# First mixer's projections taken two chunks at a time, with their weights loaded as halves of the rows

## The chip, the cores and the metric

The kernel runs on one core of one Trainium2 chip. The metric is device time in microseconds (us): three runs of the kernel before took 1580.92, 1581.1 and 1586.4 us, and their median, 1581.1 us, is the time before. One more execution was taken by the hardware profiler: it took 1579.73 us, of which 1578.0 us lie between its first and its last instruction (the span). All profile rows below come from that execution.

## The reference, cut to what matters

Two layers of a hybrid decoder run over 592 tokens at once: 16 meta tokens, 64 sample tokens (8 sequences of 8) and 512 prompt tokens. Layer 0 is an RMSNorm, one combined input projection, a group of four mLSTM heads and a group of four retention heads, an output projection, and a ConvFFN; layer 1 has another mixer. Only layer 0's input projection is touched here:

```
q_a, k_a, v_a, o_a, i_a, f_a, q_b, k_b, v_b, g_gate = split_cols(xn @ w_in, AB_SIZES)
...
xs_b = (rotary(heads(q_b, H_B), pos), rotary(heads(k_b, H_B), pos) * DK_B ** -0.5, heads(v_b, H_B))
state_b, h_b = run_blocks(ret_step, state_b, xs_b, CHUNK_B, prompt)
h_b = jax.nn.silu(g_gate.astype(jnp.float32)) * head_layer_norm(h_b, g_b)
```

`w_in` has 1024 rows and 4104 columns of four bytes. Each head of q, k, o, and of the second group's q, k and gate, has 128 columns; v has 128 columns for each head too, and i and f have four columns each.

## The kernel before, in words

Features lie on the 128 partitions and tokens on the free axis, so that activations are eight tiles of 128 x 592 (`state[0]` to `state[7]`). Every fp32 operand is kept as two tiles, a high part rounded to the fp32r format and a low part, the rest, and each product is three matmuls: high by high, high by low, low by high.

**Weights.** `raw_weights` (L346) loads a piece of a weight matrix into one of two buffers called `wr`; a piece is 512 KB in this layer. A `Split` (L281) makes of it the high part `wh` (a cast on ScalarE, L302) and the low part `wl` (a subtraction on VectorE, L306), each in one of three buffers. A `wr` buffer is free again when its `wl` has been made; a `wh` and a `wl` are free when TensorE has read them for the last time. `pump` (L321) keeps up to three pieces made and not yet used up, and `done` (L315) gives one back and makes the next. `stream` (L325) runs the dense blocks in the order of a list, and fetches ahead until two more pieces are on their way:

```
def pump():
    while line and len(live) < 3:
        line[0].get()
...
def fetch():
    while sum(len(w or ()) for w, _ in ahead) < 2:
...
S.copy(hi, src)
...
V.tensor_tensor(out=lo, in0=src, in1=hi.bitcast(F32), op=ALU.subtract)
```

**Projections.** `proj` (L417) makes one chunk of 128 output features: one piece of weights (1024 rows, 128 columns: each row of the piece is 512 bytes in memory), eight steps of `dense` (L390) of six matmuls each into one PSUM tile `dp`, and then a `post` that takes the sum out of PSUM. There are 24 such chunks in this layer: `q_`, `k_`, `o_`, `qb`, `kb` and `g_`, for four heads each. `token_proj` (L424) makes v, for two heads at once, tokens on the partitions; its weights come as two pieces of 512 rows and 256 columns (1024 bytes a row), and its results are taken out of PSUM by ScalarE, one tile of tokens at a time (L938, and L1021 for the gates' columns). There are two PSUM tiles of the size that `dp` and `tp` use.

**Mixers.** Each head has a generator, `mixer_a` (L1150) or `mixer_b` (L1245), which starts when its q and k are there (`mixer_b`: its v too) and adds its small matmuls between those of the dense blocks; at most two run at a time (`interleave`, L133). The `post` of `qb` and `kb` is `post_rot` (L1136): two copies out of PSUM on ScalarE into `sw` (L1139, L1140), then three operations on VectorE (L1142 to L1144); the last writes the k of the head, which `mixer_b` transposes on TensorE as the first thing it does (L1255, the tile `p0`). Heads of the second group are called b0 to b3 below, and those of the first a0 to a3.

**What sets the order.** The list `blocks` in `layer0` (L1314 to L1317) is written by hand. A recording layer turns the program into one in-order list of instructions for each engine, and moves instructions of the mixers between those of the dense blocks. Loads are issued from SyncE's queue (SP), which also issues the stores of states (`out_C`, `out_R`) and the loads of states (`s_s`), in order; each waits there for its buffer. ScalarE and VectorE are in order as well: a cast that waits for its load holds up what stands behind it.

Of the kernel before, what the change touches and what calls it, by code (L numbers as in the profile page):

```python
# [23 lines left out]
NT = NMETA + NSAM + NP  # L24
# [75 lines left out]
def trunk_kernel(ctx: ExitStack, tc: tile.TileContext, I, O):  # L100
# [8 lines left out]
    dp = ctx.enter_context(tc.tile_pool(name="dp", bufs=1, space=bass.MemoryType.DRAM))  # L109
# [7 lines left out]
    def matmul(out, lhsT, rhs, **kw):  # L117
        n = 1
        for d in rhs.shape[1:]:
            n *= d  # L120
        m = lhsT.shape[1]
        clock[0] += max(n, 64) / 2.4 + 3 if rhs.dtype == F32R else max(2 * n, 2 * m, 64) / 1.2
        T.matmul(out, lhsT=lhsT, rhs=rhs, **kw)  # L123
# [38 lines left out]
    def tmp(name, n=NT, dt=F32):  # L162
        return tp.tile([128, n], dt, name=name, tag="t", bufs=4)
# [10 lines left out]
    def mm(name):  # L174
        return pp.tile([128, 1024], F32, name=name, tag="mm", bufs=2)
# [29 lines left out]
    state = {"x": "xa", "h": "xb", "ssq": {}}  # L205
# [153 lines left out]
    def weights(*views):  # L359

        return [Split(r.shape[1], r.shape[2], r) for r in map(raw_weights, views)]

    def got(ws):
        return [sp.get() for sp in ws]
# [23 lines left out]
    OFF = {0: (216, 296), 14: (208, 304), 16: (208, 304)}  # L388

    def dense(ws, acts, c0=0, hooks=None, span=None):  # L390


        off, mid = OFF[c0]
        halves = [(c0, mid), (mid, NT)] if span is None else [span]
        if span is not None:
            off = -span[0]
        ps = [mm("dp") if span is None else px("dq") for _ in ws]
        nk = len(acts)
        for k in range(nk):
            xh, xl = acts[k]  # L400
            for p, (hi, lo) in zip(ps, ws):
                for i, (ww, xx) in enumerate(((hi, xh), (hi, xl), (lo, xh))):
                    for a, b in halves:
                        matmul(p[:, off + a:off + b], lhsT=ww[:, k, :], rhs=xx[:, a:b], start=k == 0 and i == 0,
                               stop=k == nk - 1 and i == 2)
            if hooks and k in hooks:
                hooks[k]()
            yield
        return ps, off

    def cols(w, c0, n=128):
        return w.rearrange("(k p) n -> p k n", p=128)[:, :, c0:c0 + n]

    def acts_x():
        return [state[c] for c in range(8)]

    def proj(w, c0, post, first=0, hooks=None):  # L417

        def body(ww):
            (p,), off = yield from dense(got(ww), acts_x(), first, hooks)  # L420
            post(p[:, off + first:off + NT])
        return (lambda: weights([cols(w, c0)]), body)

    def token_proj(w, pieces, emit, first=False, hook=None, chunks=None):  # L424

# [56 lines left out]
    def slot(kind, j, dt=F32):  # L482
        return ap.tile([128, NT], dt, name=f"{kind}{j}", tag=f"{kind}{j}")
# [51 lines left out]
    def action(f):  # L535
        def body(_):
            f()
            yield
        return (lambda: None, body)
# [393 lines left out]
    def emit_v(name):  # L933

        def f(t, r, p):
            if t == 0:
                vs[name] = vtile("v_" + name)
            S.activation(vs[name][:r, t, :, 0:128], p[:r, 0:256].rearrange("p (h d) -> p h d", d=128), AF.Copy,  # L938
                         scale=state["rt"][:r, t:t + 1])
            if t == 4:  # L940
                gates["v" + name] = True
        return f

    def gate_tile():
        return tp.tile([128, NT], F32, name="gate", tag="gate", bufs=4)

    def silu_gate(name, first=0):

        def post(p):
            z = tmp("gz")  # L950
            if first:
                G.memset(z[:, 0:first], 0.0)
            V.tensor_tensor(out=z[:, first:], in0=p, in1=state["rb"][:, first:], op=ALU.mult)
            g = gate_tile()
            S.activation(g, z, AF.Tanh, scale=0.5)
            V.scalar_tensor_tensor(out=g, in0=g, scalar=1.0, in1=z, op0=ALU.add, op1=ALU.mult)
            gates[name] = g
        return post
# [19 lines left out]
    def layer0():  # L978
        w = I["w_in_ab"][0]
# [32 lines left out]
        def emit_va(hp):  # L1012
            f0 = emit_v(f"a{hp}")

            def f(t, r, p):
                f0(t, r, p)
                if t == 0:
                    if hp == 0:
                        G.memset(gt, 0.0)
                    G.memset(vs[f"a{hp}"][:, :, :, 128:129], 1.0)  # L1020
                S.activation(gt[:r, t, 32 * hp:32 * hp + 4], p[:r, 256:260], AF.Copy, scale=state["rt"][:r, t:t + 1])  # L1021
            return f
# [91 lines left out]
        def post_q(h):  # L1114
            def f(p):
                q = slot("bh", h)
                V.tensor_tensor(out=q, in0=p, in1=state["rb"], op=ALU.mult)
                qk["q", h] = q
            return f

        def post_k(h):
            def f(p):
                k = slot("bl", h)
                V.scalar_tensor_tensor(out=k, in0=p, scalar=128 ** -0.5, in1=state["rb"], op0=ALU.mult, op1=ALU.mult)
                qk["k", h] = k
            return f

        def post_o(h):
            def f(p):
                g = gate_tile()  # L1130
                V.tensor_tensor(out=g, in0=p, in1=state["rb"], op=ALU.mult)
                S.activation(g, g, AF.Tanh, scale=0.5)
                gates["a", h] = g
            return f

        def post_rot(h, sc, kind, key):  # L1136
            def f(p):
                sw = tmp("sw")
                S.copy(sw[0:64, :], p[64:128, :])  # L1139
                S.copy(sw[64:128, :], p[0:64, :])  # L1140
                t1 = slot(kind, 4 + h)
                V.scalar_tensor_tensor(out=t1, in0=p, scalar=sc, in1=cosr, op0=ALU.mult, op1=ALU.mult)  # L1142
                V.scalar_tensor_tensor(out=sw, in0=sw, scalar=sc, in1=sinr, op0=ALU.mult, op1=ALU.mult)
                V.tensor_tensor(out=t1, in0=t1, in1=sw, op=ALU.add)  # L1144
                qk[key, 4 + h] = t1
            return f
# [98 lines left out]
        def mixer_b(h):  # L1245
# [54 lines left out]
            for t, (t0, r) in enumerate(TILES[1:]):  # L1300
# [3 lines left out]
            S.copy(nums[:, 1:5, 0:128], quad(na))  # L1304
            mixed[4 + h] = yield from head_out(nums, epst[:, h, :], gate_mul, 4 + h, gnh[:, 4 + h:5 + h], True, ("b", h))

        q_ = lambda h: proj(w, 128 * h, post_q(h))
        k_ = lambda h: proj(w, 512 + 128 * h, post_k(h))
        o_ = lambda h: proj(w, 1536 + 128 * h, post_o(h))
        qb = lambda h: proj(w, 2056 + 128 * h, post_rot(h, 1.0, "bh", "q"))  # L1310
        kb = lambda h: proj(w, 2568 + 128 * h, post_rot(h, 128 ** -0.5, "bl", "k"))
        g_ = lambda h: proj(w, 3592 + 128 * h, silu_gate(("b", h)))
        vb = lambda hp: token_proj(w, [(3080 + 256 * hp, 256)], emit_v(f"b{hp}"))
        blocks = [token_proj(w, [(1024, 256), (2048, 4)], emit_va(0), first=True, chunks=start),  # L1314
                  token_proj(w, [(1280, 256), (2052, 4)], emit_va(1), hook=norm_bcast), action(setup),
                  q_(0), k_(0), q_(1), k_(1), o_(0), q_(2), k_(2), o_(1), q_(3), k_(3), o_(2), vb(0),
                  qb(0), kb(0), o_(3), qb(1), kb(1), g_(0), vb(1), qb(2), kb(2), g_(1), qb(3), kb(3), g_(2), g_(3)]  # L1317
        streams = [rows()] + [mixer_a(h) for h in range(4)] + [mixer_b(h) for h in range(4)]
        return blocks, streams, mixed

# [302 lines left out]
    def finish(a, b):  # L1623
# [22 lines left out]
        for c in range(0, 8, 2):  # L1646
# [5 lines left out]
            ld.dma_start(out=O["y"][:, c:c + 2, a - NMETA:b - NMETA], in_=y)  # L1652

    b0, s0, mix0 = layer0()
    b1, s1, mix1 = layer1()
    blocks = b0 + mix_proj(I["w_out_ab"][0], mix0, 0, V_NFFN, xin)
# [65 lines left out]
```

## Time and profile before

| | |
|---|---|
| median of three runs | 1581.1 us (1580.92 to 1586.4) |
| the profiled execution | 1579.73 us |
| its span | 1578.0 us |
| TensorE matmuls busy | 1530.4 us, 97% of the span |
| weight loads into TensorE busy | 1483.8 us, 94% |
| VectorE busy | 1148.9 us, 73% |
| ScalarE busy | 730.9 us, 46% |
| GpSimd busy | 194.2 us, 12% |
| mean granted TensorE clock | 0.992 of full speed |

A busy share is an average over stages with different limits. The first mixer takes about the first 305 us of the span; the 24 projections lie between 47 and 302 us. To see what a change in it can be worth, one reads what TensorE waited for in that stretch, which engine ended each wait, and what that engine had waited for before. Idle time is given in brackets before an instruction, with what ended it.

### The profile page before, as it was taken

What the parts mean: (1) busy time and instruction counts of PE and PEld (TensorE: products, weight loads), DVE (VectorE), ACT (ScalarE), POOL (GpSimd) and SP (SyncE); (2) the same over time, 40 slices, a digit from 0 to 9 for tenths busy, and PEclk for the clock granted to TensorE, in tenths of its full rate; (3) what the DMA queues carried; (4) which work ended last, traced back from release to release, by engine and by line L of the source; (5) the groups of instructions that cost most, each with busy time, mean ns of one, the idle gap of its engine ahead of it and who ended that gap; (6) DMA issues with size and microseconds to landing.
All of it is one profiled execution on the core that took longest, in us unless ns stands there. A gap on an engine that the chain in (4) does not pass through costs nothing. (4 is left out here: it accounts for less than half of the span.)

```text
span 1578.0 us, 32152 instructions
## 1 busy us (share of the span) xinstructions
PE 1530.4 (97%) x13100; PEld 1483.8 (94%) x13100; DVE 1148.9 (73%) x2359; ACT 730.9 (46%) x1325; POOL 194.2 (12%) x399
## 2 busy tenths in 40 slices
PE   7999999999999999999998899999999999999996
PEld 7999998999999999999998798898999999999995
DVE  6576573758988877777556776766689887888875
ACT  6443343335444444444355556564454444444453
POOL 2000000001210000110004525333012000000001
PEclk9999999999999999999999999999999999999998
DMA  6654556423322232223422132123333223233234
GB/s 185 98 98 87 92 101 64 132 82 100 89 80 82 83 93 81 86 88 118 152 81 67 57 97 99 57 97 99 98 99 94 81 81 93 82 95 93 69 108 131
DMA packets 217812, 148.57 MB, mean 94 GB/s; under 512 B 7704, under 2 KB 209176, under 8 KB 217664
## 3 DMA queue, kind: packets, MB, share of 16 engines
q1 hardware_dynamic: 217664, 146.51, 34.7%
q8 instruction: 103, 1.69, 0.4%
q14 instruction: 45, 0.37, 0.1%
HBM read 131.84 MB, written 14.65 MB: 93 GB/s over the span
## 5 line engine op out<-in xcount | busy, mean ns | idle before, releaser
L302 ACT CAST wh<-wr 128x1024 fp32r<-128x1024 f32 (+3 forms) x238 | 230.7, 970 | 394.1 <-PE dp L123 118.5
L306 DVE TENSOR_TENSOR wl<-wr,wh 128x1024 fp32r<-128x1024 f32 (+3 forms) x238 | 267.9, 1126 | 75.4 <-ACT wh L302 73.2
L123 PE MATMUL dp<-h,wh 128*128 128x296 f32 (+1 forms) x1088 | 242.4, 304 | 0.7 <-ACT v_c L938 0.5
L123 PE MATMUL dp<-xl,wh 128*128 128x296 f32 (+1 forms) x1088 | 236.6, 298 | 0.0
L123 PE MATMUL dp<-h,wl 128*128 128x296 f32 (+1 forms) x1088 | 236.4, 298 | 0.0
L123 PE MATMUL dp<-bh,wh 128*128 128x296 f32 (+2 forms) x864 | 188.4, 299 | 0.8 <-DVE x L511 0.5
L123 PE MATMUL dp<-bh,wl 128*128 128x296 f32 (+2 forms) x864 | 186.5, 297 | 0.0
L123 PE MATMUL dp<-bl,wh 128*128 128x296 f32 (+2 forms) x864 | 186.4, 297 | 0.0
L123 PEld LDWEIGHTS dp<-h,wh 128*128 128x128 f32 x1088 | 174.5, 189 | 4.3 <-issue 1.8
L123 PEld LDWEIGHTS dp<-xl,wh 128*128 128x128 f32 x1088 | 176.7, 189 | 0.0
L123 PEld LDWEIGHTS dp<-h,wl 128*128 128x128 f32 x1088 | 176.3, 188 | 0.0
L123 PEld LDWEIGHTS dp<-bh,wh 128*128 128x128 f32 x864 | 139.0, 188 | 3.1 <-issue 1.4
L123 PEld LDWEIGHTS dp<-bh,wl 128*128 128x128 f32 x864 | 139.5, 188 | 0.0
L123 PEld LDWEIGHTS dp<-bl,wh 128*128 128x128 f32 x864 | 139.4, 188 | 0.0
L123 PE MATMUL ac<-h,wh 128*128 128x296 f32 (+1 forms) x408 | 123.3, 302 | 2.6 <-DVE cs L724 2.6
L123 PE MATMUL ac<-h,wl 128*128 128x296 f32 (+1 forms) x408 | 121.5, 298 | 0.0
L123 PE MATMUL ac<-xl,wh 128*128 128x296 f32 (+1 forms) x408 | 121.3, 297 | 0.0
L123 PE MATMUL tp<-wh,h 128*128 128x256 f32 (+3 forms) x280 | 82.8, 300 | 12.8 <-ACT wh L298 6.0
L615 ACT ACTIVATE cv<-cv 128x612 f32<-128x612 f32 (+1 forms) x44 | 31.1, 708 | 116.9 <-DVE cv L611 116.9
L302 ACT CAST wh<-s 128x1024 fp32r<-128x1024 f32 x68 | 56.8, 835 | 59.0 <-PE sb L123 34.7
L123 PEld LDWEIGHTS ac<-h,wh 128*128 128x128 f32 x408 | 76.9, 188 | 5.1 <-DVE cs L724 3.9
L123 PE MATMUL sb<-b2h,wl 128*128 128x296 f32 (+1 forms) x272 | 81.0, 298 | 0.0
(475 smaller groups left out, 3431.9 us busy)
## 6 DMA issues: line engine op xcount, KB each, us to landing
wr<-in_w_ffn_in SPq DMA_DIRECT2D x88, 512.0 KB, 3.8
wr<-in_w_ffn_out SPq DMA_DIRECT2D x32, 512.0 KB, 3.5
wr<-in_w_in_c SPq DMA_DIRECT2D x32, 512.0 KB, 3.9
wr<-in_w_in_ab SPq DMA_DIRECT2D x30, 512.0 KB, 7.6
wr<-in_w_ffn_out SPq DMA_DIRECT2D x24, 384.0 KB, 3.5
x<-in_x SPq DMA_DIRECT2D x16, 296.0 KB, 4.2
out_H<-s_s SPq DMA_DIRECT2D x8, 576.0 KB, 2.8
wr<-in_w_out_ab SPq DMA_DIRECT2D x16, 256.0 KB, 2.7
```

Of the source, the lines that this page charges most:

```text
L123: T.matmul(out, lhsT=lhsT, rhs=rhs, **kw)
L302: S.copy(hi, src)
L306: V.tensor_tensor(out=lo, in0=src, in1=hi.bitcast(F32), op=ALU.subtract)
L615: S.activation(env_["cv"][:, b0:612], env_["cv"][:, b0:612], AF.Silu)
```

## The change

A new function `proj_pair` takes two neighbouring chunks, 256 columns, as one block. Their weights come as two pieces as before, but cut the other way: the upper 512 rows and the lower 512 rows, 256 columns each, so that a row of a piece is 1024 bytes. The pieces stay 512 KB, the casts and subtractions stay of the same size and number (24 each), and so do the matmuls. The first chunk goes through the steps 0 to 7. The second goes through 4 to 7 and then 0 to 3, so that the piece of the steps 4 to 7 is used up after three quarters of the block, where `done` gives it back. Both pieces must be made before the block's instructions are written down; on the chip, the matmuls of a step wait only for the piece that they read.

The list of blocks follows: the heads of q, k, o, qb, kb and g now come in pairs of heads (0, 1) and (2, 3), so that q of head 1 comes before k of head 0, and so on; `vb(0)` stays behind k of head 3 but moves ahead of o of head 2, and `vb(1)` stands behind the gates of heads 0 and 1.

```
--- before.py
+++ after.py
@@ -420,6 +420,27 @@
             (p,), off = yield from dense(got(ww), acts_x(), first, hooks)
             post(p[:, off + first:off + NT])
         return (lambda: weights([cols(w, c0)]), body)
+
+    def proj_pair(w, c0, posts):
+
+
+        def body(ws):
+            halves = got(ws)
+            off, mid = OFF[0]
+            for i, ks in enumerate((range(8), (4, 5, 6, 7, 0, 1, 2, 3))):
+                p = mm("dp")
+                for k in ks:
+                    hi, lo = (w_[:, k % 4, 128 * i:128 * i + 128] for w_ in halves[k // 4])
+                    xh, xl = state[k]
+                    for j, (ww, xx) in enumerate(((hi, xh), (hi, xl), (lo, xh))):
+                        for a, b in ((0, mid), (mid, NT)):
+                            matmul(p[:, off + a:off + b], lhsT=ww, rhs=xx[:, a:b], start=k == ks[0] and j == 0,
+                                   stop=k == ks[-1] and j == 2)
+                    if i and k == 7:
+                        ws[1].done()
+                    yield
+                posts[i](p[:, off:off + NT])
+        return (lambda: weights(*[[cols(w, c0, 256)[:, k0:k0 + 4, :]] for k0 in (0, 4)]), body)
 
     def token_proj(w, pieces, emit, first=False, hook=None, chunks=None):
 
@@ -1304,17 +1325,17 @@
             S.copy(nums[:, 1:5, 0:128], quad(na))
             mixed[4 + h] = yield from head_out(nums, epst[:, h, :], gate_mul, 4 + h, gnh[:, 4 + h:5 + h], True, ("b", h))
 
-        q_ = lambda h: proj(w, 128 * h, post_q(h))
-        k_ = lambda h: proj(w, 512 + 128 * h, post_k(h))
-        o_ = lambda h: proj(w, 1536 + 128 * h, post_o(h))
-        qb = lambda h: proj(w, 2056 + 128 * h, post_rot(h, 1.0, "bh", "q"))
-        kb = lambda h: proj(w, 2568 + 128 * h, post_rot(h, 128 ** -0.5, "bl", "k"))
-        g_ = lambda h: proj(w, 3592 + 128 * h, silu_gate(("b", h)))
+        def two(c0, post):
+            return lambda h: proj_pair(w, c0 + 128 * h, [post(h), post(h + 1)])
+
+        q_, k_, o_ = two(0, post_q), two(512, post_k), two(1536, post_o)
+        qb = two(2056, lambda h: post_rot(h, 1.0, "bh", "q"))
+        kb = two(2568, lambda h: post_rot(h, 128 ** -0.5, "bl", "k"))
+        g_ = two(3592, lambda h: silu_gate(("b", h)))
         vb = lambda hp: token_proj(w, [(3080 + 256 * hp, 256)], emit_v(f"b{hp}"))
         blocks = [token_proj(w, [(1024, 256), (2048, 4)], emit_va(0), first=True, chunks=start),
                   token_proj(w, [(1280, 256), (2052, 4)], emit_va(1), hook=norm_bcast), action(setup),
-                  q_(0), k_(0), q_(1), k_(1), o_(0), q_(2), k_(2), o_(1), q_(3), k_(3), o_(2), vb(0),
-                  qb(0), kb(0), o_(3), qb(1), kb(1), g_(0), vb(1), qb(2), kb(2), g_(1), qb(3), kb(3), g_(2), g_(3)]
+                  q_(0), k_(0), o_(0), q_(2), k_(2), vb(0), qb(0), o_(2), kb(0), g_(0), vb(1), qb(2), kb(2), g_(2)]
         streams = [rows()] + [mixer_a(h) for h in range(4)] + [mixer_b(h) for h in range(4)]
         return blocks, streams, mixed
 
```

Three places show how it moves instructions. The first is SyncE's queue from the last state stores of the heads b0 and b1 on. Before, `wr_2722`, `wr_2724`, `wr_2877`, `wr_2939`, `wr_3001`, `wr_3186` and `wr_3262` are the weights of qb(2), kb(2), g(1), qb(3), kb(3), g(2) and g(3), and `wr_3324` is the first of the output projection:

```order
L355 DMA wr_2724<-in_w_in_ab 128x8x128
L1298 DMA out_R<-s_s_2550 128x1152
L355 DMA wr_2877<-in_w_in_ab 128x8x128
L969 DMA s_s_3339<-in_R0 128x1024
L355 DMA wr_2939<-in_w_in_ab 128x8x128
L355 DMA wr_3001<-in_w_in_ab 128x8x128
L355 DMA wr_3186<-in_w_in_ab 128x8x128
L355 DMA wr_3262<-in_w_in_ab 128x8x128
L1298 DMA out_R<-s_s_3014 128x1152
L355 DMA wr_3324<-in_w_out_ab 128x4x128
```

Now `wr_2796` and `wr_2798` are the two pieces of qb(2) and qb(3), `wr_2951` and `wr_2953` those of kb(2) and kb(3), and `wr_3075` and `wr_3077` those of g(2) and g(3):

```order
L355 DMA wr_2796<-in_w_in_ab 128x4x256
L990 DMA s_s_3146<-in_R0 128x1024
L1319 DMA out_R<-s_s_2552 128x1152
L990 DMA s_s_3339<-in_R0 128x1024
L355 DMA wr_2798<-in_w_in_ab 128x4x256
L355 DMA wr_2951<-in_w_in_ab 128x4x256
L355 DMA wr_2953<-in_w_in_ab 128x4x256
L355 DMA wr_3075<-in_w_in_ab 128x4x256
L355 DMA wr_3077<-in_w_in_ab 128x4x256
L355 DMA wr_3324<-in_w_out_ab 128x4x128
```

In these rows two pieces stood ahead of the load `s_s_3339` before and four pieces of the projections behind it; now one piece stands ahead of it and five behind.

The second place is ScalarE in the same stretch, the casts and the copies of `post_rot`. Before, `sw_2994` is that of kb(2), and the cast ahead of it is that of kb(3)'s weights, `wr_3001`:

```order
L302 CAST wh_2879<-wr_2877 128x1024
L302 CAST wh_2941<-wr_2939 128x1024
L1139 COPY sw_2932<-dp_2883 64x592
L1140 COPY sw_2932<-dp_2883 64x592
L302 CAST wh_3003<-wr_3001 128x1024
L1139 COPY sw_2994<-dp_2945 64x592
L1140 COPY sw_2994<-dp_2945 64x592
L852 ACTIVATE hi_3037<-p0_3023,csm_74 80x128
```

Now `sw_3132` is that of kb(2), `sw_3068` that of qb(3):

```order
L302 CAST wh_2955<-wr_2951 128x1024
L1160 COPY sw_3008<-dp_2959 64x592
L1161 COPY sw_3008<-dp_2959 64x592
L302 CAST wh_3040<-wr_2953 128x1024
L302 CAST wh_3079<-wr_3075 128x1024
L1160 COPY sw_3068<-dp_3015 64x592
L1161 COPY sw_3068<-dp_3015 64x592
L1160 COPY sw_3132<-dp_3083 64x592
L1161 COPY sw_3132<-dp_3083 64x592
L302 CAST wh_3207<-wr_3077 128x1024
L873 ACTIVATE hi_3169<-p0_3155,csm_74 80x128
```

The copies of kb(2) no longer stand directly behind a cast; two casts now stand together ahead of the copies of qb(3).

The third place is TensorE where the head b2 starts, with the transpose of its k (`p0`). Before, it comes 32 matmuls into the next block, g(1), `dp_3007` (the rows before these are of the same block):

```order
L123 MATMUL dp_3007<-h4_143,wh_2879 128x296 x2
L123 MATMUL dp_3007<-xl4_144,wh_2879 128x296 x2
L123 MATMUL dp_3007<-h4_143,wl_2881 128x296 x2
L123 MATMUL dp_3007<-h5_154,wh_2879 128x296 x2
L127 MATMUL p0_3023<-csm_74,bl6_2997 80x128
L123 MATMUL p0_3023<-bh6_2935,bl6_2997 80x80
L127 MATMUL kp_3022<-csm_74,bl6_2997 128x128 x4
L123 MATMUL sp_3021<-bh6_2935,bl6_2997 128x128 x4
```

Now it comes 27 matmuls into the block's second chunk, kb(3), `dp_3139`:

```order
L123 MATMUL dp_3139<-h7_176,wh_3040 128x296 x2
L123 MATMUL dp_3139<-xl7_177,wh_3040 128x296 x2
L123 MATMUL dp_3139<-h7_176,wl_3042 128x296 x2
L123 MATMUL dp_3139<-h0_100,wh_2955 128x296 x2
L123 MATMUL dp_3139<-xl0_101,wh_2955 128x296
L127 MATMUL p0_3155<-csm_74,bl6_3135 80x128
L123 MATMUL p0_3155<-bh6_3011,bl6_3135 80x80
L127 MATMUL kp_3154<-csm_74,bl6_3135 128x128 x4
L123 MATMUL sp_3153<-bh6_3011,bl6_3135 128x128 x4
```

The distance from the end of kb(2) to the first reader of its result shrank by five matmuls. For the head b3, it was 29 matmuls and is 19, with 14 matmuls of b2's last stage in addition between the two; for b0, it was 32 and is 27, and for b1, 32 and 26.

## Rows read from the trace of the kernel before

**Rows 1.** Windows of core 0: stretch, its us, busy us and count by engine, clock, DMA
```profile
60.00:245.00 185.00, 184.10 (x1424) 172.94 (x1424) 119.16 (x390) 75.42 (x169) 1.34 (x7) 1.00 0.52 91
```
**Rows 2.** Waits of TensorE from 60 to 310 us: total us, times, longest
```profile
PE p L127 <- DVE bl L1144: 3.8, 4, 3.3
PE p L127 <- DVE zq L839: 0.5, 1, 0.5
```
**Rows 3.** Timeline of TensorE around the first wait: start, us, what, idle before
```profile
36.24 0.28 PE L123 MATMUL tp<-wh,xl 128*128 128x260 f32 x1
...
36.95 0.28 PE L123 MATMUL tq<-wh,xl 128*128 128x260 f32 x1
40.86 0.58 PE L123 MATMUL tp<-wh,h 128*128 128x260 f32 x1 [3.64 <-ACT gtd L1021]
```
**Rows 4.** Timeline of ScalarE ahead of the first wait's end
```profile
31.29 0.41 ACT L862 ACTIVATE ve<-v_a,csm 80x128 fp32r<-80x128 f32 x1
35.66 1.05 ACT L302 CAST wh<-wr 128x1024 fp32r<-128x1024 f32 x1 [3.96 <-DMA wr<-in_w_in_ab]
...
40.20 0.47 ACT L938 ACTIVATE v_a<-tp,rt 128x256 f32<-128x256 f32 x1
40.55 0.26 ACT L1021 ACTIVATE gtd<-tp,rt 128x4 f32<-128x4 f32 x1
```
**Rows 5.** DMA issues from 23 to 26.3 us, q(0)'s weights: size, us to landing
```profile
wr<-in_w_in_ab SPq DMA_DIRECT2D x1, 512.0 KB, 9.7
```
**Rows 6.** DMA from 27 to 32 us: packets, MB, share of the 16 engines' time
```profile
q1 hardware_dynamic: 815, 0.41, 63.7%
```
**Rows 7.** Windows of core 0 behind the first wait; the clock is third from the end
```profile
41.00:43.00 2.00, 2.00 (x10) 2.00 (x11) 0.00 (x0) 0.00 (x0) 0.00 (x0) 0.50 1.04 57
43.00:45.00 2.00, 2.00 (x15) 2.00 (x15) 0.00 (x0) 0.00 (x0) 0.00 (x0) 0.79 0.98 197
```
**Rows 8.** Timeline of TensorE, first matmuls of b0 and of b2, and the end of each
```profile
190.67 0.31 PE L127 MATMUL p<-csm,bl 128*80 128x128 f32 x1 [0.15 <-DVE bl L1144]
...
195.62 0.52 PE L123 MATMUL dp<-xl,wh 128*128 128x296 f32 x2
...
265.05 0.30 PE L127 MATMUL p<-csm,bl 128*80 128x128 f32 x1 [3.25 <-DVE bl L1144]
...
271.59 0.52 PE L123 MATMUL dp<-xl,wh 128*128 128x296 f32 x2
```
**Rows 9.** Timeline of ScalarE ahead of the second wait's end
```profile
260.32 1.05 ACT L302 CAST wh<-wr 128x1024 fp32r<-128x1024 f32 x1 [5.57 <-DMA wr<-in_w_in_ab]
261.39 0.65 ACT L1139 COPY sw<-dp 64x592 f32<-64x592 f32 x1
```
**Rows 10.** DMA issues from 247 to 248 us, kb(3)'s weights
```profile
wr<-in_w_in_ab SPq DMA_DIRECT2D x1, 512.0 KB, 13.1
```
**Rows 11.** DMA from 247 to 260 us
```profile
q1 hardware_dynamic: 2696, 1.36, 95.1%
```
**Rows 12.** DMA from 210 to 216 us: qb(2)'s weights alone, 512-byte rows
```profile
q1 hardware_dynamic: 1040, 0.52, 50.8%
...
wr<-in_w_in_ab SPq DMA_DIRECT2D x1, 512.0 KB, 5.6
```
**Rows 13.** DMA from 125 to 131 us: a piece of vb(0), 1024-byte rows
```profile
q1 hardware_dynamic: 528, 0.52, 45.0%
...
wr<-in_w_in_ab SPq DMA_DIRECT2D x1, 512.0 KB, 5.2
```
**Rows 14.** Timeline of TensorE in a block: two starts, 24 matmuls apart
```profile
50.28 0.43 PE L123 MATMUL dp<-h,wh 128*128 128x296 f32 x2
...
53.55 0.43 PE L123 MATMUL dp<-h,wh 128*128 128x296 f32 x2
```
**Rows 15.** Groups by form, 60 to 310 us: busy, mean ns, idle before and its releasers
```profile
L302 ACT CAST wh<-wr 128x1024 fp32r<-128x1024 f32 x24 | 25.2, 1048 | 61.2 <-PE dp L123 28.9 <-DMA wr<-in_w_in_ab 27.3 <-issue 4.2
...
L306 DVE TENSOR_TENSOR wl<-wr,wh 128x1024 fp32r<-128x1024 f32 x25 | 30.5, 1219 | 40.8 <-ACT wh L302 40.7
```

## The prediction

> **What bounds the kernel now.** I first read the windows of the first mixer, to see which engine is full. From 60 to 245 us TensorE is busy for 184.10 of 185 us at full clock [rows 1]: in that stretch only fewer or shorter matmuls could save much, and the change keeps all of them. So I looked for what TensorE waits for. From 60 to 310 us its waits come to 4.3 us, 3.8 of them for the k of a head of the second group, and one such wait alone is 3.3 [rows 2]. Ahead of 60 us the timeline shows another of 3.64 us [rows 3]. These two are what a change of projections can win; each was followed back over the engines.
>
> The first wait, at 37.2 us: the third token tile of v has no PSUM buffer until ScalarE has taken out the second, whose last matmul ends at 36.24 + 0.28 = 36.52 [rows 3]. ScalarE does so only from 40.20 to 40.55 + 0.26 = 40.81, because ahead of it in its queue stands the cast of the weights of q(0), which waits 3.96 us for its load, until 35.66 [rows 4]. That load took 9.7 us [rows 5], so it was issued at about 26.0. From 27 to 32 us the queue moved 815 packets in 5 us, 163 per us, with the DMA engines busy 63.7% of the time [rows 6]; the load has 1024 packets of 512 bytes. After the wait TensorE's granted clock, full (2.4 GHz) up to then, is 0.50 for 2 us and 0.79 for another 2 [rows 7]: 2 x 0.50 + 2 x 0.21 = 1.4 us lost.
>
> The second wait, 3.25 us at 265.05, is the first matmul of b2, which reads the k that kb(2)'s post writes [rows 8]. That post begins with two copies of 0.65 us on ScalarE, from 261.39, and in front of them stands the cast of kb(3)'s weights, which had waited 5.57 us for its load, until 260.32 [rows 9]. This load took 13.1 us [rows 10]. From 247 to 260 us the DMA engines are 95.1% busy, with 2696 packets and only 1.36 MB, some 500 bytes each [rows 11]: 13 x 16 x 0.951 / 2696 = 73 ns of an engine for a packet. The head b2 then needs 271.59 - 265.05 = 6.54 us for what b0 did in 195.62 - 190.67 = 4.95 [rows 8], so 1.6 us went to a lower clock. The head b0, whose cast had its weights in time, waited 0.15 us.
>
> **What the change moves in these two places.** A piece now has 512 packets of 1024 bytes. The nearest rows: qb(2)'s weights on an almost idle queue take 5.6 us, 6 x 16 x 0.508 / 1040 = 47 ns a packet [rows 12]; a piece of v with 1024-byte rows takes 5.2 us, 6 x 16 x 0.450 / 528 = 82 ns [rows 13]. For a piece of 512 KB that is 1024 x 47 / 16 = 3.0 us of all engines for short rows when alone, 1024 x 73 / 16 = 4.7 in the crowded stretch, and 512 x 82 / 16 = 2.6 for long rows: a gain between 13% and 45%.
>
> First wait. At the 163 packets per us of [rows 6], 512 packets are through in 3.1 us, at 30.1 if they begin at 27, and landed by about 31.5. ScalarE has finished its earlier work at 31.29 + 0.41 = 31.70, so the cast would not wait [rows 4]. If bytes and not packets set the pace, the load lands at 35.66 as before. I take the packets, since the engines were not full there. Everything behind the cast then moves up by 3.96 us, but no further than the end of the second tile's matmuls, 36.52, plus 0.6 us of taking out: about 0.3 us of the wait stays. Gain 3.64 - 0.3 = 3.3, bounds 0 and 3.6; and with it the 1.4 us of clock, since what is left is near b0's 0.15, behind which the clock held.
>
> Second wait. Kb(2)'s copies no longer stand behind a cast that needs a fresh load: the two pieces of the next block are cast ahead of qb(3)'s copies, a chunk earlier, and kb(3) needs no weights of its own. In the order the last loads have 62 to 74 matmuls between issue and cast; a step of 6 matmuls takes (53.55 - 50.28) / 4 = 0.82 us [rows 14], so 0.136 us a matmul and 8.5 to 10 us, where the load behind the one that was late had 39, 5.3 us. Gain 3.25 - 0.15 = 3.1, bounds 0 and 3.25, and 1.6 of clock.
>
> **What it adds.** The transposes of the four heads come sooner after their k: 27, 26, 27 and 19 matmuls instead of 32, 32, 32 and 29. Five matmuls are 0.7 us, and the slack was nothing (b0 waited 0.15 already). So each head waits up to 0.7 us more, but ScalarE may also be free sooner. Between 0 and 4 x 0.65 = 2.6 I take 0.5, nearer to zero, since ahead of the copies of b0 and b2 now stands no cast with a fresh load.
>
> At nothing: the 24 casts and the subtractions stay as many and as large, 1.05 and 1.22 us [rows 15], and run beside TensorE. The lower piece of a block, released by the early hand-back at three quarters of the block before, has 36 to 55 matmuls, 4.9 to 7.5 us, up to its first use, and cast and subtraction take 2.3 of it; without that cover each block would wait at its fifth step. The loads of states pass one place of SyncE's queue and find their buffers free. Heads of the first group end up to two chunks later, in a stretch with projections enough.
>
> **The sum.** -(3.3 + 1.4 + 3.1 + 1.6) + 0.5 = -8.9 us. The profiled execution, 1579.7, becomes 1570.8; against the median, 1581.1, that is **1572.2**, or 0.56% less. About 0.5%, 7.9 us, is what a measurement of this kernel can tell from no change; the forecast lies just past it.
>
> **The rivals.** *Only the second wait goes.* For it: by bytes the early load lands no sooner, and the loads of states and tables beside it stay. -(3.1 + 1.6) + 0.5 = -4.2, so 1576.9. Chance 0.20.
>
> *The length of a row changes nothing.* For it: 5.2 against 5.6 us when the queue is quiet [rows 12, 13]; against it the 73 ns of [rows 11]. The first wait stays, and the second one, with the queue as full as before, is only handed to the block behind: +0.5, so 1581.6. Chance 0.10. The Trainium skill, "DMA: Bandwidth & Descriptors", section Specifications, speaks for this one: transfers reach line rate from 512 bytes on. By that rule the weights had line rate before the change and nothing would be won; the trace does not bear it out in the stretch of 95.1%, where 512-byte rows came to 105 GB/s, and no row here shows what longer ones would have come to in it.
>
> *Crowding.* Heads b2 and b3, a2 and a3, now get their q and k as neighbours, so two mixers run in the same blocks, and the copies, casts and mixers' work on ScalarE and VectorE meet. For it: b3 has 14 matmuls of b2's last stage just ahead of it. Two new waits of the size of the second, 3.25 + 1.6 each, are 9.7 us, -8.9 + 9.7 = +0.8: 1581.9. Chance 0.12.
>
> *Late lower halves: slower.* At the fifth step of each block, TensorE reads the second piece. Its cast may start only when the hand-back has come and ScalarE is there; if mixers hold ScalarE or VectorE for over 4.9 - 2.3 = 2.6 us in that stretch, TensorE stands. It decides from there on. For it: casts idled 27.3 us behind loads and 28.9 behind TensorE, over 24 of them [rows 15], so the chain is not slack on every block. Against it: nearly all idle time there is spare, as TensorE is full [rows 1]. In half of the 12 blocks, 6 x 4.85 = 29 us, less 8.9: 1601. Chance 0.08. The forecast keeps 0.50.
>
> **How the numbers follow.** The forecast's own range is 1569 (no new cost, no rest of the first wait, and 0.5 of the other wait in [rows 2], with the scatter of a few tenths) to 1575 (an early wait cut by only half). The range 1569.0 to 1583.0 takes in the first three rivals, with 1.1 us above 1581.9 for heads that wait longer than 0.5 in all, and leaves out the late halves and the ends of the others, some 0.15. Faster by over 0.5% means below 1573.2: four fifths of the forecast, 0.40. Slower by over 0.5%: the late halves, 0.08. The rest, 0.52, is within.
>
> **What would show it.** Right: the wait of 3.64 us is at most 0.4, b2 waits under 0.8 us, the granted clock stays full at 41 to 45 and 265 to 269 us, casts idle behind loads for much less than 27.3 us, and kb's and g's loads land in some 5 us. Wrong: waits of TensorE at a block's fifth step on a high or low part, new waits on the k of b1 or b3, another fall of the clock, or an early cast that still waits for its load past 33 us.

## The result, and the profile after

The changed kernel takes **1572.84 us**, the median of four runs (1571.81 to 1574.36). The kernel before, run beside it, had a median of 1583.75 us (four runs, 1580.92 to 1587.12). The ratio is 0.994, with an interval from 0.9916 to 0.9963: a gain of 0.6%, where 1572.2 us and 0.56% were forecast. A second set of six runs gave 1573.06 us and 0.9939 (0.9925 to 0.9953).

| | before | after |
|---|---|---|
| span of the profiled execution | 1578.0 us | 1571.5 us |
| TensorE matmuls busy | 1530.4 us | 1529.4 us |
| first matmul of q(0) | 47.31 us | 44.82 us |
| last of the mixer's heads leaves ScalarE | 315.69 us | 308.06 us |
| waits of TensorE from 60 to 310 us | 4.3 us | none |
| longest wait of TensorE ahead of q(0) (third token tile of v) | 3.64 us | 1.76 us |
| median landing of this matrix's loads | 7.6 us | 5.9 us |

The busy time of TensorE did not fall; its waits did. The gain lies where it was sought: the mixer ends 315.69 - 308.06 = 7.6 us sooner, of which 47.31 - 44.82 = 2.5 lie ahead of q(0) and 5.1 behind its first matmul; the rest of the program is longer by 1.1 us, which no run explains.

The first wait, to be read against [rows 3]. The timeline of TensorE in the changed kernel:

```profile
36.91 0.28 PE L123 MATMUL tp<-wh,xl 128*128 128x260 f32 x1
...
37.62 0.28 PE L123 MATMUL tq<-wh,xl 128*128 128x260 f32 x1
39.66 0.39 PE L123 MATMUL tp<-wh,h 128*128 128x260 f32 x1 [1.76 <-ACT gtd L1042]
```

and ScalarE ahead of it, against [rows 4]:

```profile
34.45 1.05 ACT L302 CAST wh<-wr 128x1024 fp32r<-128x1024 f32 x1 [2.08 <-DMA wr<-in_w_in_ab]
...
38.99 0.46 ACT L959 ACTIVATE v_a<-tp,rt 128x256 f32<-128x256 f32 x1
39.35 0.26 ACT L1042 ACTIVATE gtd<-tp,rt 128x4 f32<-128x4 f32 x1
```

The cast of q's first piece still waits for its load, 2.08 us instead of 3.96, and the evacuation that TensorE needs still stands behind it. The load itself got shorter, from 9.7 us [rows 5] to 6.3, in the DMA issues from 28 to 29 us:

```profile
wr<-in_w_in_ab SPq DMA_DIRECT2D x1, 512.0 KB, 6.3
```

What came back in full is the clock. The windows behind the first wait, against [rows 7], and two in the tail (the clock is third from the end):

```profile
41.00:43.00 2.00, 2.00 (x19) 2.00 (x18) 0.00 (x0) 0.15 (x1) 0.00 (x0) 1.00 0.56 210
43.00:45.00 2.00, 2.00 (x19) 2.00 (x18) 0.35 (x1) 1.53 (x3) 0.00 (x0) 1.00 0.00 0
265.00:267.00 2.00, 2.00 (x17) 2.00 (x16) 1.65 (x3) 0.00 (x0) 0.16 (x2) 1.00 1.00 123
267.00:269.00 2.00, 2.00 (x16) 2.00 (x16) 0.00 (x0) 0.20 (x1) 0.32 (x3) 1.00 0.38 108
```

It is at full rate where 0.50 and 0.79 stood behind the first wait. In the tail this stood before:

```profile
265.00:267.00 2.00, 1.95 (x13) 1.95 (x14) 0.60 (x3) 1.25 (x3) 0.00 (x0) 0.68 1.01 55
267.00:269.00 2.00, 2.00 (x19) 1.59 (x18) 1.00 (x2) 1.28 (x4) 0.00 (x0) 0.50 1.01 54
```

There the casts no longer wait for loads either. The group of casts from 60 to 310 us, against [rows 15]:

```profile
L302 ACT CAST wh<-wr 128x1024 fp32r<-128x1024 f32 x24 | 25.1, 1047 | 34.5 <-PE dp L123 31.3 <-issue 1.7 <-PE tp L123 0.7
```

The 27.3 us behind loads are gone; what is left is waiting for TensorE to give buffers back, which costs nothing. And the transfer engines have room where they had none [rows 11]; DMA from 250 to 260 us:

```profile
q1 hardware_dynamic: 1056, 1.05, 64.3%
...
wr<-in_w_in_ab SPq DMA_DIRECT2D x2, 512.0 KB, 6.7
```

That looks like the forecast to the letter. The experiments show that one of its reasons, the number of packets, was not what made the loads shorter.

### The profile page after: what moved, and what is told of

Read it like the earlier page. It is cut to its first block, busy times and chain, and to the rows that moved or that the text cites. A ratio compares the mean times of both kernels' runs of the same rounds, so it can differ in the third digit from the quotient of the medians.

```text
span 1571.5 us, 32162 instructions
## 1 busy us (share of the span) xinstructions
PE 1529.4 (97%) x13100; PEld 1482.5 (94%) x13100; DVE 1147.1 (73%) x2359; ACT 731.1 (47%) x1325; POOL 193.7 (12%) x399
## 5 line engine op out<-in xcount | busy, mean ns | idle before, releaser
L123 PE MATMUL tp<-wl,h 128*128 128x256 f32 (+3 forms) x280 | 80.7, 289 | 0.5 <-DVE wl L299 0.5
```

## The experiments

All ratios are to the kernel before, run on the same chip in the same set.

**The order alone** (`e1`): single chunks and old loads, in the order of pairs.

```
- q_(0), k_(0), q_(1), k_(1), o_(0), q_(2), ...
+ q_(0), q_(1), k_(0), k_(1), o_(0), o_(1), q_(2), q_(3), k_(2), k_(3), vb(0), qb(0), qb(1), o_(2), o_(3), ...
```

> The new order of the projections with the old pieces (one chunk, 1024 rows of 512 bytes each). Theory (row length matters for how long a load takes, the order only for where it falls): loads of these weights stay near 7.6 us, q(0)'s load comes as late as before and the early wait stays at 2 to 4 us; in the tail one load still has 39 matmuls, 5.3 us, from issue to cast, so casts wait for loads by 5 us or more in all; a third to a half of the gain is left, ratio 0.996 to 1.000. Rival A (the order did it all): the ratio equals that of the whole change, 0.994, casts wait for loads less than 3 us. Rival B (the order does harm alone): above 1.001, with new waits on the k of the second group's heads of 3 us or more.

Measured: 1588.3 us, ratio 1.0038 (1.0026 to 1.0051). The order by itself does harm, so rival B. TensorE's waits from 60 to 310 us; then ScalarE ahead of the wait of 2.8 us at 274.28, and ahead of the longest, at 289.59; then the DMA from 263 to 266 us:

```profile
PE dp L123 <- DVE bh L1142: 5.4, 2, 2.8
PE p L127 <- DVE bl L1144: 4.4, 2, 4.2
```
```profile
270.95 1.05 ACT L302 CAST wh<-wr 128x1024 fp32r<-128x1024 f32 x1 [11.06 <-DMA wr<-in_w_in_ab]
272.02 0.65 ACT L1139 COPY sw<-dp 64x592 f32<-64x592 f32 x1
...
284.86 1.05 ACT L302 CAST wh<-wr 128x1024 fp32r<-128x1024 f32 x1 [7.71 <-DMA wr<-in_w_in_ab]
285.94 0.65 ACT L1139 COPY sw<-dp 64x592 f32<-64x592 f32 x1
```
```profile
q1 hardware_dynamic: 309, 0.16, 104.0%
```

Both are the old second wait again, the longest of them larger: a cast that waits for its load, the copies of a head behind it, and TensorE behind these. While two such loads are on their way the transfer engines are full with 0.16 MB in 3 us, 54 GB/s: 3 x 16 x 1.04 / 309 = 161 ns of an engine for a packet of 512 bytes.

**Short rows in the changed kernel** (`e2`): each half by two transfers of 128 columns.

```
-        return (lambda: weights(*[[cols(w, c0, 256)[:, k0:k0 + 4, :]] for k0 in (0, 4)]), body)
+        return (lambda: weights(*[[cols(w, c0 + c)[:, k0:k0 + 4, :] for c in (0, 128)] for k0 in (0, 4)]), body)
```

> The changed kernel with every half of a pair loaded by two transfers of 128 columns (rows of 512 bytes), buffers, casts and order unchanged. Theory (row length): the loads take over 7 us instead of 5.9, the transfer engines are busy for over 0.8 of the crowded stretch from 250 to 260 us instead of 0.64, casts wait for loads again (10 us or more in all from 60 to 310), the early wait is above 2.5 us; ratio 0.996 to 1.000. Rival (512 bytes are enough, only the order and the halves matter): loads take within 0.5 us of those of the change, TensorE waits nowhere from 60 to 310 us, ratio within 0.002 of the change.

Measured: 1573.02 us, ratio 0.994 (0.9926 to 0.9954), no wait of TensorE from 60 to 310 us. The rival holds in its time and its waits (its loads, of half the size, cannot be compared one by one): the length of a row is not what makes the gain. DMA from 250 to 260 us, and the early wait:

```profile
q1 hardware_dynamic: 2090, 1.04, 67.1%
```
```profile
38.82 0.39 PE L123 MATMUL tp<-wh,h 128*128 128x260 f32 x1 [2.59 <-ACT gtd L1042]
```

Twice the packets of the changed kernel take hardly more of the engines: 10 x 16 x 0.671 / 2090 = 51 ns for 512 bytes, where the change needs 10 x 16 x 0.643 / 1056 = 97 ns for 1024. My step from "half the packets" to "half the time" was wrong. Of the theory one point came true, the early wait of over 2.5 us; casts do wait for loads, but by 5.4 us where 10 were expected, and TensorE does not wait behind them.

**Without the early hand-back** (`e3`).

```
-                    if i and k == 7:
-                        ws[1].done()
```

> The changed kernel without the early hand-back of the second piece. The second piece of a block is then cast when the block before has ended, with 24 matmuls, 3.3 us, before its first use; cast and subtraction take 2.3 us, with two copies of 0.65 us ahead of them for the second group. Theory (the hand-back is what covers the second piece): TensorE waits at the fifth step of most blocks, 0.3 to 1.5 us each, 4 to 12 us in all from 60 to 310, ratio 0.996 to 1.002. Rival (3.3 us are cover enough): waits under 1 us in all, ratio as the change.

Measured: 1571.81 us, ratio 0.9935 (0.9915 to 0.9955), no wait from 60 to 310 us. The theory fell, and with it the prediction's rival of the late lower halves: 24 matmuls of cover are enough, and the hand-back may go. The edit changes nothing ahead of q(0), so this profile is also another start of the change. In it the tiles of v started as early as before, and the first wait is almost gone:

```profile
37.65 0.39 PE L123 MATMUL tp<-wh,h 128*128 128x260 f32 x1 [0.37 <-ACT gtd L1040]
```

**Two transfers for each old piece** (`e4`), and **the same with every second piece turned** (`e5`): the kernel before, with

```
+            for k0 in ((4, 0) if turn[0] else (0, 4)):
+                ld.dma_start(out=raw[:, k0:k0 + 4, :], in_=cols(w, c0)[:, k0:k0 + 4, :])
```

where `turn[0]` stays 0 in the first and alternates in the second.

> The kernel before, order and rows of 512 bytes unchanged, but each chunk's piece (1024 rows of 128 columns) comes by two transfers of 512 rows. The runs so far say that row length is not the cause: short rows in halves do as well as long ones, while a piece of 1024 rows in one transfer takes 11 to 13 us where two are on their way together, at 54 GB/s with the transfer engines full. Theory A (one long transfer of 1024 rows is the slow form): split in two, the load of kb(3)'s weights takes under 8 us instead of 13.1, b2 waits under 1 us instead of 3.25, and half of the gain of the change or more is there, ratio 0.994 to 0.997. Theory B (two loads that go over the same rows of the matrix at the same time, at different columns, slow each other): nothing changes, over 10 us, b2 waits over 2 us, ratio 0.998 to 1.002.

> As the kernel with two transfers for each piece, but every second piece takes the lower 512 rows first, so that two pieces on their way together are at different rows. Theory A (one long transfer is the slow form): as the kernel with two transfers. Theory B (the same rows at the same time): the loads now take under 8 us where two go together, b2 waits under 1 us, ratio 0.994 to 0.997, and the kernel with two transfers stays at 0.998 or above. Theory C (only the time from issue to cast matters, 39 matmuls against 62 here): both stay at 0.998 or above, with casts that wait for loads 20 us or more in all from 60 to 310 us.

Measured: 0.9992 (0.9981 to 1.0002) and 0.9987 (0.9975 to 0.9998). Neither form helps by more than a trace. Casts waited for loads 26.0 us in both. Theories A and B fall, theory C stands. The DMA from 250 to 260 us in the first of them, and its early wait:

```profile
q1 hardware_dynamic: 2010, 1.00, 99.1%
```
```profile
41.86 0.59 PE L123 MATMUL tp<-wh,h 128*128 128x260 f32 x1 [5.52 <-ACT gtd L1032]
```

Against the short rows in halves, this has packets of the same 512 bytes and transfers of the same 256 KB, but 10 x 16 x 0.991 / 2010 = 79 ns a packet instead of 51. One difference is which transfers follow each other: there the two take neighbouring columns of the same rows, here the same columns of other rows. The order of the projections and the times of issue differ as well.

**Pairs from the same rows** (`e7`): in the changed kernel, every second pair goes through the rows the other way.

```
-            for i, ks in enumerate((range(8), (4, 5, 6, 7, 0, 1, 2, 3))):
+            for i, ks in enumerate(((4, 5, 6, 7, 0, 1, 2, 3), range(8)) if f else (range(8), (4, 5, 6, 7, 0, 1, 2, 3))):
...
-        return (lambda: weights(*[[cols(w, c0, 256)[:, k0:k0 + 4, :]] for k0 in (0, 4)]), body)
+        return (lambda: weights(*[[cols(w, c0, 256)[:, k0:k0 + 4, :]] for k0 in ((4, 0) if f else (0, 4))]), body)
```

> The changed kernel, where every second pair goes through the rows the other way (steps 4 to 7 and 0 to 3, then 0 to 7, its lower piece loaded first), so that the last piece of a pair and the first of the next, which are on their way together, come from the same 512 rows. Theory B (the same rows at the same time): the loads that go together from 245 to 262 us take over 9 us instead of 6.3 to 7.1, the transfer engines are full at under 70 GB/s there, ratio 0.995 to 1.000. Theory A (the long transfer) or C (time from issue to cast): loads within 1 us of those of the change, no wait of TensorE from 60 to 310 us, ratio as the change, 0.994.

Measured: 1573.42 us, ratio 0.9945 (0.9927 to 0.9963). DMA from 250 to 260 us:

```profile
q1 hardware_dynamic: 971, 0.96, 57.1%
...
wr<-in_w_in_ab SPq DMA_DIRECT2D x2, 512.0 KB, 6.9
```

Loads as before, so theory B is out from this side too.

**A third buffer in the kernel before** (`e8`): old order, old loads, one more piece on its way.

```
-        while sum(len(w or ()) for w, _ in ahead) < 2:
+        while sum(len(w or ()) for w, _ in ahead) < 3:
-            raw = wp.tile([128, k, n], F32, name="wr", tag="wr", bufs=2)
+            raw = wp.tile([128, k, n], F32, name="wr", tag="wr", bufs=3)
```

and, for the room, 3 instead of 4 buffers `t` and 6 instead of 7 buffers `s`.

> The kernel before, its order and its loads unchanged (one transfer of 1024 rows, 512 bytes each), with a third buffer for loaded weights and one more piece fetched ahead; two other pools give a buffer each to make room. The load that had 39 matmuls, 5.3 us, from issue to cast now has 87, 12 us. Theory C (a load is late because it is issued late; its own length counts only against that time): hardly a cast waits for a load from 60 to 310 us, under 5 us in all, the wait of b2 goes, though loads still take 8 to 13 us; ratio 0.993 to 0.996. Rival (with more loads on their way they slow each other, as two together do): loads over 13 us, casts wait as before, ratio 0.998 or above.

Measured: 1576.05 us, ratio 0.9968 (0.9956 to 0.9981), a third of a per cent; the forecast of 0.993 to 0.996 was too good, since the early wait stays. In the tail, more time from issue to cast is shown to be enough. The DMA from 252 to 253 us, TensorE's only wait from 60 to 310 us, the group of casts there, and the early wait:

```profile
q1 hardware_dynamic: 107, 0.05, 106.3%
...
wr<-in_w_in_ab SPq DMA_DIRECT2D x1, 512.0 KB, 13.2
```
```profile
PE p L127 <- DVE bl L1144: 0.2, 1, 0.2
```
```profile
L302 ACT CAST wh<-wr 128x1024 fp32r<-128x1024 f32 x24 | 25.2, 1048 | 56.7 <-PE dp L123 51.7 <-issue 4.2 <-PE tp L123 0.7
```
```profile
39.72 0.58 PE L123 MATMUL tp<-wh,h 128*128 128x260 f32 x1 [3.82 <-ACT gtd L1021]
```

Loads are as slow as before, one takes 13.2 us with the engines full, and no cast waits for one: issued 87 matmuls ahead or more, they have 12 us and up. At the start the third buffer does not help: q(0)'s cast still waits 4.87 us for its load.

**Pairs in the tail only** (`e10`): q, k and the first two of o in single chunks and the old order.

```
+ q1_(0), k1_(0), q1_(1), k1_(1), o1_(0), q1_(2), k1_(2), o1_(1), q1_(3), k1_(3),
+ vb(0), qb(0), o_(2), kb(0), g_(0), vb(1), qb(2), kb(2), g_(2)]
```

> Pairs and their order for qb, kb and g and the last two of o alone; q, k and the first two of o in single chunks and the old order. The first wait should stay at 3 us or more with its fall of the clock, the second go: half of the gain, 4 to 5.5 us, ratio 0.9965 to 0.9975. If the gain of the tail is more than the wait and the clock behind it, the ratio is below 0.996; if the halves at the start made the tail good by shifting its loads, it is above 0.998.

Measured: 1577.97 us, ratio 0.9983 (0.9972 to 0.9993): 0.7 to 2.8 parts in a thousand, 1.1 to 4.4 us, less than the 4 to 5.5 us that were expected; and 0.9983 lies above the 0.998 that was to mean that the halves at the start made the tail good. From 60 to 310 us one wait of 1.1 us is left, not on a head's k. At the start it stands as before:

```profile
41.71 0.59 PE L123 MATMUL tp<-wh,h 128*128 128x260 f32 x1 [3.76 <-ACT gtd L1042]
```

The traces do not bear that meaning out. They can be split at the first matmul of q(0), which is behind the first wait and begins the 24 chunks:

| profile | first matmul of q(0) | from there to the mixer's last head |
|---|---|---|
| before | 47.31 us | 268.4 us |
| the change | 44.82 us | 263.2 us |
| the change without hand-back (`e3`) | 42.79 us | 263.2 us |
| the kernel before in the new order (`e1`) | 49.87 us | 276.1 us |
| the kernel before with a third buffer (`e8`) | 47.34 us | 262.8 us |
| pairs in the tail only (`e10`) | 48.18 us | 263.8 us |

With pairs in the tail only, 4.6 of the 5.1 us behind q(0) are there without the halves at the start; this profile's start is 0.9 us later, which hides some of it in the time. So by the traces the stretch behind q(0) is worth 5.1 us and the start 2.5, or 4.5 in the profile of `e3`. The medians, 1583.75 - 1572.84 = 10.9 and 1582.39 - 1573.06 = 9.3 us, are larger than the 7.6 us between the two profiles; the profiled execution of the kernel before, 1579.73, was faster than all four of its runs in the first set.

**A later cast** (`e6`): in the changed kernel, q's first cast is asked for only behind the third token tile.

```
+                if room[0] == 2 and t == 2:
+                    room[0] = 3
+                    pump()
```

> The changed kernel with the cast of q's first piece put behind the evacuation of the third token tile in ScalarE's queue, where it can no longer hold it up. If the cast that waits for its load is all that is left of the first wait, the wait of TensorE near 39.7 us falls from 1.76 to under 0.5 us and the time by 1 to 1.5 us (ratio about 0.993). Rival: the second piece's load, which waits for the first one's buffer, comes later by 3 us, and TensorE waits at the fifth step of q's first chunk instead, 0.5 to 2 us: time as the change or slightly above.

Measured: 1572.3 us, ratio 0.9939 (0.9922 to 0.9955). It tells nothing of the cast: the recording layer put the cast back to where it stood on ScalarE, and its wait with it:

```profile
32.74 1.05 ACT L302 CAST wh<-wr 128x1024 fp32r<-128x1024 f32 x1 [2.24 <-DMA wr<-in_w_in_ab]
```

**The change with a third buffer** (`e9`): both edits together.

> The changed kernel with the third buffer as well. From 60 to 310 us nothing is left to win, so what changes is the start: the loads of the second v block and of q's first piece are issued sooner, and the wait of 1.76 us near 39.7 us goes. 1 to 3 us less than the change, ratio 0.992 to 0.994. Rival (loads that come sooner take the transfer engines from the tokens' own loads in the first 20 us): the first matmuls come later by as much, ratio as the change or above; or the missing temporaries cost something elsewhere.

Measured: 1568.86 us (1566.86 to 1569.68), ratio 0.992 (0.9907 to 0.9934), below all ten runs of the change (1571.46 at the least). The early wait, which was to go, is down to 1.04 us:

```profile
37.03 0.39 PE L123 MATMUL tp<-wh,h 128*128 128x260 f32 x1 [1.04 <-ACT gtd L1042]
```

This is the fastest version that was run, though its interval overlaps that of the change in its second set, 0.9925 to 0.9953. Its mixer ends 2.5 us before that of the change in the second profile of that one, and all of it lies ahead of q(0), at 42.19 instead of 44.79 us. But `e3` and `e7`, with two buffers, had q(0) at 42.79 and 42.77, so one profile does not show that the third buffer did it.

> The changed kernel once more, for the scatter of its start-up and as the partner of the runs beside it. Theory (both waits were loads that came late, and the change ends them for good): no wait of TensorE from 60 to 310 us, no cast that waits for a load in that stretch, ratio to the kernel before 0.992 to 0.997. Rival (the profile of the change fell on a lucky start): the early wait for the evacuation of a token tile is back at 3 us or more, with the clock at 0.50 behind it, and the ratio is above 0.998.

That is the second set of six runs, 0.9939. In its profile the early wait is 1.96 us, and neither TensorE nor a cast waits for a load from 60 to 310 us, as in the first: for that stretch the theory held. At the start a load still comes late.

## Why the prediction was right, and where it was not

*The second wait* (3.1 and 1.6 of clock): gone, and the clock stays full; both terms came as forecast in the trace. Behind q(0)'s first matmul the change takes 5.1 us less, where these two and the 0.5 us of the other wait in [rows 2] come to 5.2. Of its two reasons, the time from issue to cast is enough by itself when it is 12 us and more: then even loads of 13 us cost nothing (`e8`). In the change it is 8.5 to 10 us by the prediction's count. A load of 13 us would still be late there, so that its loads are shorter, 6.7 us, is part of the gain; but they are not shorter for having fewer packets (`e2`). No run has the change's times of issue with loads as slow as before, so the shares of the two reasons stay open. Two readings were wrong and change nothing in the sum: the load with 39 matmuls is that of qb(3), ahead of the late one and not behind it, and the two casts ahead of qb(3)'s copies are the lower piece of kb's block and the upper one of g's.

*The first wait* (3.3): 1.9 us of it in the profile of the change, as a rest of 1.76 us stayed where 0.3 was forecast; with short rows the rest is 2.59. "I take the packets, since the engines were not full there" was a wrong reason, as the short rows of the tail show, but the load did get shorter, by 3.4 us. In this profile it was also issued later, at 34.45 - 6.3 = 28.1 instead of 26.0, as the tiles ahead of it started later. In `e3`, where they started as before, the cast began at 32.44 and the rest was 0.37: there the term is right. So its size hangs on a start-up that the prediction took as fixed. *Its clock* (1.4): right, at 41 to 45 us. Yet it need not come back: in `e6`, behind a wait of 1.90 us, it was 0.61 and 0.53 from 38 to 42 us. The prediction calls the clock full up to the first wait; it was 0.72 in the mean from 26 to 32 us before, and 1.00 after. That is no gain of the change, as `e3` had 0.50 from 28 to 30 us again.

*The sum* (8.9): 7.6 us by the two profiles up to the end of the mixer, 9.7 with the start of `e3`, 9.3 and 10.9 by the medians. That 1572.2 came within 0.7 us of 1572.84 is in part luck: the profiles of the changed start alone have q(0) anywhere from 42.8 to 45.5 us, and the runs of the kernel before go from 1577.3 to 1587.1.

*The added 0.5* for transposes that come sooner: nothing showed; no head waited for its k. This makes up for part of what the first wait kept.

*The rival that row length changes nothing* was right in its premise and wrong in its end, 1581.6: it took the second wait to hang on row length. By the Trainium skill, "DMA: Bandwidth & Descriptors", section Specifications, transfers reach line rate from 512 bytes on. The run with short rows in halves agrees in time, 0.994 both ways; the 54 GB/s of 512-byte rows in `e1` show that such rows do not always get it.

*Crowding* and *late halves* did not show, the second not even without the hand-back.

What stays open: why 512-byte packets cost 51 ns when neighbouring columns are asked for together, 79 when not, and 161 at worst. That it is the nearness of what is read is argued from two runs that differ in the order of the projections too; no run changes it alone.

## What to carry to other kernels

A load that is late is a matter of two times, how long it takes and how far ahead of its reader it is issued. Here the tail could be mended by the second alone, and the start was not mended by a buffer more. Test them apart, by the same bytes in another form, and by one more buffer with the same loads. Fewer and larger packets shorten a load only if packets set its pace, which a share of busy engines does not tell. And an in-order engine that casts for one consumer and evacuates for another turns a late load of the first into a wait of the second.

## What the runs showed of the hardware

Sixteen full transfer engines moved anything from 54 GB/s (`e1`) to 100 GB/s (`e4`) with packets of the same size. A busy share of 95% is no sign that the bytes are too many.

TensorE's clock stayed at full rate (2.4 GHz) behind waits of 1.42 and 1.76 us in the change and of 1.96 us in its second profile. It fell behind 1.90 us in `e6` (0.61 and 0.53 from 38 to 42 us), around 2.59 us in `e2` (0.81 from 36 to 41 us, 0.62 from 41 to 43) and behind 3.82 us in `e8` (0.50, that is 1.2 GHz, from 41 to 45). In the kernel before it was at 0.50 from 28 to 30 us, behind two waits of 0.94 and 0.57 us close together. So the length of one wait does not tell these cases apart.
